# First products of a two-layer trunk: four plain output tiles while x loads, sums of x behind them, pairs in another order

## The chip, the core and the metric

The kernel runs on one core of a Trainium2 chip. The metric is the device time of one execution, in microseconds (us). Five engines work side by side, each with its own queue that is worked off in order: TensorE (PE) multiplies matrices, VectorE (DVE), ScalarE (ACT) and GpSimd (POOL) do elementwise work, and SyncE (SP) issues nearly all DMAs.

## What is computed

A block of 512 tokens x of width 2048 goes through two layers, all in float32. The first is a gated pooling mixer; the second is a latent attention layer that this change does not touch.

```
h = rmsnorm(x, norm_g)
proj = h @ w_in                          # 2048 x 8192
u, gate = proj[..., :4096], proj[..., 4096:]
pooled = causal_mean_pool(u, w) - u      # four groups of 1024, w = 2, 4, 8, 16
y = einsum(pooled, w_group) * scale      # per group 1024 x 1024
y = y * silu(gate)
x = x + y @ w_out
# then shared keys and values, attention with a gate, out projection
```

## The kernel before, in words

Activations lie transposed: 128 channels on the partitions and the 512 tokens along the free axis, so x is 16 tiles (`xT`), and the input product has 64 output tiles of 128 channels, numbers 0 to 31 for u and 32 to 63 for the gate. The rms factor of x is one number per token, so the product runs on x times its gain (`C_GA`) and the factor `ra` is multiplied in afterwards.

Every product is made in split precision. A float32 operand is cast to `hi` (ACT) and its remainder `lo` = value minus hi is made on DVE; three matmuls hi·hi, hi·lo and lo·hi add up in PSUM. In code lines these are a group of three.

The input product saves matmuls by a seven-multiplication scheme for 2x2 blocks (`SEVEN`, `seven`). A **pair** is two output tiles; a step j takes two tiles of x (2j and 2j+1), each in two halves of H = 256 tokens. So a pair and a step make a 2x2 times 2x2 block product, with seven products of 256 columns in place of eight, each in three matmuls: a pair has 8 steps x 7 x 3 = 168 matmuls. It needs sums of weights and sums of x:

- `x_combos(j)` loads two tiles of x, scales them on ACT into a buffer `raw` of eight slots (L275, L277), forms four sums on DVE (L279 to L282), casts seven slots to `xh` (L283) and makes `xl` (L284). These stay for the whole product.
- `w_combos(pair, q)` loads the weights of two steps (L290, two DMAs), forms sums on DVE (L293) and on POOL (L295, L296), casts seven slots (L299) and makes lo (L300). The buffer `raw` has three copies, hi and lo two each.
- `gather` adds the products of a pair up from PSUM into two output tiles and stores them to DRAM (`raws`). The second tile of a pair comes out negated. For u tiles 0 to 7 it applies the pooling window 2 first, which needs `ra`.

The first two pairs, 16 and 17 (gate tiles 32 to 35), run side by side step by step while x is loaded and combined (L353 to L364), in all eight PSUM banks. Then come pairs 18 and 19, then 0 to 15 (u), then 20 to 31 (gates). `squares`, called in pair 18, loads all of x again, squares it on ACT and adds on POOL (L348); `norm_r` in pair 19 makes `ra` from it.

After the product, `pooled_tile` and `y_tile` read `raws` back, group by group, and the group and out products follow (`proj`), with 512-column matmuls at L139, L140 and L141. Their weights are cast at L121 and subtracted at L122.

What sets the order: the code is recorded, and a scheduler with a cost model of its own sorts the instructions of each engine and gives out pool buffers. So instructions stand on an engine in another order than in the code, and wait for semaphores in that order. Memory pools are opened and closed as a stack; a tile in a pool that is opened later waits for the tiles that lay there.

Of the kernel before, what the change touches and what calls it, by code (L numbers as in the profile page):

```python
# [51 lines left out]
def trunk_kernel(  # L52
# [31 lines left out]
    def bt(shape=(P, S), dt=F32R):  # L84
        return bpool.tile(list(shape), dt, tag="b", name="bt")

    def tt_(n=S, dt=F32):
        return tpool.tile([P, n], dt, tag="t", name="tt_")

    def mm():  # L90
        return ps.tile([P, S], F32, tag="mm", name="mm", bufs=3)
# [7 lines left out]
    def f(ap):  # L99
        return ap.bitcast(F32)  # L100

    def dram():
        return dpool.tile([P, S], F32, tag="scr", name="scr", bufs=64)
# [119 lines left out]

    H = 256
    NJ = KD // 2
    raws = [None] * (2 * WA // P)
    ra = [None]

    def pool_tile(src, neg, w):
# [25 lines left out]

    with ExitStack() as c1:
        xcp = c1.enter_context(tc.tile_pool(name="xcp", bufs=NJ))
        epool = c1.enter_context(tc.tile_pool(name="epool", bufs=2))
        w7 = c1.enter_context(tc.tile_pool(name="w7", bufs=2))
        ps7 = c1.enter_context(tc.tile_pool(name="ps7", bufs=2, space=bass.MemoryType.PSUM))  # L260
        xh, xl = [None] * NJ, [None] * NJ

        def raw8():
            return w7.tile([P, 8, H], F32, tag="raw", name="raw", bufs=3)

        def x_combos(j):
            xa, xb_ = tt_(), tt_()
            nc.sync.dma_start(xa, xT[2 * j])
            nc.sync.dma_start(xb_, xT[2 * j + 1])
            h = xcp.tile([P, 7, H], F32R, tag="xh", name="xh")  # L270
            lo = xcp.tile([P, 7, H], F32R, tag="xl", name="xl")
            xh[j], xl[j] = h, lo
            c = raw8()

            A.activation(c[:, 6:8, :].rearrange("p h t -> p (h t)"), xa, AF.Copy,  # L275
                         scale=cs[:, C_GA + 2 * j:C_GA + 2 * j + 1])
            A.activation(c[:, 0:2, :].rearrange("p h t -> p (h t)"), xb_, AF.Copy,  # L277
                         scale=cs[:, C_GA + 2 * j + 1:C_GA + 2 * j + 2])
            V.tensor_tensor(c[:, 2, :], c[:, 6, :], c[:, 7, :], ALU.subtract)  # L279
            V.scalar_tensor_tensor(c[:, 3, :], c[:, 2, :], -1.0, c[:, 1, :], ALU.mult, ALU.subtract)  # L280
            V.scalar_tensor_tensor(c[:, 4, :], c[:, 3, :], -1.0, c[:, 0, :], ALU.mult, ALU.subtract)
            V.tensor_tensor(c[:, 5, :], c[:, 1, :], c[:, 7, :], ALU.subtract)  # L282
            A.copy(h, c[:, 0:7, :])  # L283
            V.tensor_tensor(lo, c[:, 0:7, :], f(h), ALU.subtract)  # L284

        def w_combos(pair, q):

            c = w7.tile([P, 2, 8, P], F32, tag="raw", name="raw", bufs=3)
            for m in range(2):
                nc.sync.dma_start(c[:, :, 2 - 2 * m:4 - 2 * m, :],  # L290
                                  awin[2 * pair + m][:, q * S:(q + 1) * S].rearrange(
                                      "p (j k n) -> p j k n", j=2, k=2))
            V.tensor_tensor(c[:, :, 4:6, :], c[:, :, 0:1, :].broadcast_to([P, 2, 2, P]),  # L293
                            c[:, :, 1:3, :], ALU.add)
            G.tensor_tensor(c[:, :, 6, :], c[:, :, 4, :], c[:, :, 2, :], ALU.add)  # L295
            G.tensor_tensor(c[:, :, 7, :], c[:, :, 6, :], c[:, :, 3, :], ALU.add)  # L296
            hi = w7.tile([P, 2, 7, P], F32R, tag="hi", name="hi")
            lo = w7.tile([P, 2, 7, P], F32R, tag="lo", name="lo")
            A.copy(hi, c[:, :, 1:8, :])  # L299
            V.tensor_tensor(lo, c[:, :, 1:8, :], f(hi), ALU.subtract)  # L300
            return hi, lo

        def banks():
            return [ps7.tile([P, 2, H], F32, tag=f"k{i}", name=f"k{i}") for i in range(4)]


        SEVEN = ((2, 0, 0, 0), (0, 4, 1, 0), (1, 6, 2, 0), (3, 2, 3, 0),
                 (5, 3, 0, 1), (6, 1, 1, 1), (4, 5, 2, 1))

        def seven(ks, w, j):  # L310
            hi, lo = w
            for wi, xi, b, h in SEVEN:
                dst = ks[b][:, h, :]
                first, last = j == 0 and h == 0, j == NJ - 1

                T.matmul(dst, hi[:, j % 2, wi, :], xh[j][:, xi, :], start=first, stop=False,  # L316
                         skip_group_check=True)
                T.matmul(dst, hi[:, j % 2, wi, :], xl[j][:, xi, :], start=False, stop=False,  # L318
                         skip_group_check=True)
                T.matmul(dst, lo[:, j % 2, wi, :], xh[j][:, xi, :], start=False, stop=last,  # L320
                         skip_group_check=True)

        def gather(ks, pair):

            e = epool.tile([P, 7, H], F32, tag="e", name="e")
            A.copy(e[:, 6, :], ks[2][:, 0, :])
            V.tensor_tensor(e[:, 0:2, :], e[:, 6:7, :].broadcast_to([P, 2, H]), ks[0], ALU.add)
            V.tensor_tensor(e[:, 2, :], e[:, 1, :], ks[2][:, 1, :], ALU.add)
            V.tensor_tensor(e[:, 3:6:2, :], e[:, 1:3, :], ks[3][:, 0:1, :].broadcast_to([P, 2, H]), ALU.add)
            V.tensor_tensor(e[:, 4:7:2, :], e[:, 2:4, :], ks[1], ALU.add)  # L330
            for i, v in enumerate((e[:, 0:7:6, :], e[:, 4:6, :])):
                o = 2 * pair + i
                raws[o] = dram()
                if o < 8:
                    nc.sync.dma_start(raws[o], pool_tile(v, i == 1, WINS[0]))
                else:
                    nc.sync.dma_start(raws[o].rearrange("p (h t) -> p h t", h=2), v)

        def squares():
            accs = [tt_(), tt_()]  # L340
            for k in range(KD):
                x = tt_()
                nc.sync.dma_start(x, xT[k])
                if k < 2:
                    A.activation(accs[k], x, AF.Square)
                else:
                    A.activation(x, x, AF.Square)
                    G.tensor_tensor(accs[k % 2], accs[k % 2], x, ALU.add)  # L348
            V.tensor_tensor(accs[0], accs[0], accs[1], ALU.add)
            return accs[0]  # L350


        k0, k1 = banks(), banks()  # L353
        for j in range(NJ):
            x_combos(j)
            if j % 2 == 0:
                wa = w_combos(16, j // 2)
                wb = w_combos(17, j // 2)
                continue
            for i in (j - 1, j):  # L360
                seven(k0, wa, i)
                seven(k1, wb, i)
        gather(k0, 16)
        gather(k1, 17)  # L364
        ss = None
        for pair in (18, 19, *range(16), *range(20, 32)):
            ks = banks()
            for q in range(NJ // 2):
                w = w_combos(pair, q)
                seven(ks, w, 2 * q)  # L370
                seven(ks, w, 2 * q + 1)
            if pair == 18:
                ss = squares()
            if pair == 19:
                p = ps7.tile([P, 2, H], F32, tag="k3", name="k3").rearrange("p h t -> p (h t)")
                ra[0] = norm_r(ss, D, p)
            gather(ks, pair)

    tile_ = dict(reuse_waits="tile")
    wpool = ctx.enter_context(tc.tile_pool(name="wpool", bufs=3, **tile_))  # L380
    apool = ctx.enter_context(tc.tile_pool(name="apool", bufs=32, **tile_))
    bpool = ctx.enter_context(tc.tile_pool(name="bpool", bufs=32, **tile_))
    xpool = ctx.enter_context(tc.tile_pool(name="xpool", bufs=16, **tile_))
    ps = ctx.enter_context(tc.tile_pool(name="ps", bufs=2, space=bass.MemoryType.PSUM, **tile_))


# [2 lines left out]
    def pooled_tile(g, o):  # L389
        x = tt_()  # L390
        nc.sync.dma_start(x, raws[g * 8 + o])
        if g:
            x = pool_tile(x, o % 2 == 1, WINS[g])
        hi, lo = at(), at()
        split(x, hi, lo)
        return hi, lo

    def y_tile(g, o, pooled):
        z = tt_()
        nc.sync.dma_start(z, raws[32 + g * 8 + o])  # L400
        V.scalar_tensor_tensor(z, z, -1.0 if o % 2 else 1.0, ra[0], ALU.mult, ALU.mult)
        A.activation(z, z, AF.Silu)
        acc2 = proj(awg[g, o], 8, pooled)
        c = C_ASC + g * 8 + o
# [499 lines left out]
```

## Time and profile before

| | us |
|---|---|
| median of 3 runs | 1993.39 (1992.2 to 1994.09) |
| the profiled execution | 1993.23 |
| its span, first to last instruction | 1991.4 |
| PE busy | 1941.2 (97%), 11372 matmuls |
| DVE busy | 1289.7 (65%) |
| ACT busy | 815.8 (41%) |
| POOL busy | 299.1 (15%) |

The profile is that of one execution. Busy time counts an instruction from start to end; matmuls overlap, so their pitch (from start to start) is shorter than the time that one is shown with. The granted clock is the share of full speed at which TensorE ran. In rows of the timeline stand start, duration, engine, line, operation, output<-inputs and shape, and in brackets the idle time ahead of it and what ended it. A wait is put down to what came last.

### The profile page before, as it was taken

To read this page: it belongs to the slowest core of one execution; us is meant where nothing else is said; L and a number is where in the kernel's file an instruction comes from. 1 tells how busy PE (TensorE), PEld (TensorE's weight loads), DVE (VectorE), ACT (ScalarE), POOL (GpSimd) and SP (SyncE) were. 2 spreads that over 40 slices of the span, in tenths; PEclk is the share of its full clock that TensorE was granted. 3 is DMA by queue.
4 is the path that set the end of the run, shared out by engine and by line. 5 is a ranking of instruction groups with operands and counts; after the bars stand their busy time and mean duration, and the time that the engine had idled before them with its cause. 6 is when DMAs were issued, how large, how long until landed. Compare 5 with 4: busy or idle time off the path is not lost.

```text
span 1991.4 us, 30647 instructions
## 1 busy us (share of the span) xinstructions
PE 1941.2 (97%) x11372; PEld 1717.5 (86%) x11372; DVE 1289.7 (65%) x2291; ACT 815.8 (41%) x1527; POOL 299.1 (15%) x434
## 2 busy tenths in 40 slices
PE   5699999999999999999999999999999999999999
PEld 5699999999999978888888888888888788878887
DVE  6778866666666589377496567473344878787422
ACT  5433333333333353233333354233244767675221
POOL 2733432222222200000000000000010211110000
PEclk9799999999999999999999999999999999999999
DMA  4534544444444374344344344323332111121632
GB/s 157 175 111 134 168 129 138 128 135 125 135 127 134 121 243 159 106 127 148 112 128 136 107 144 132 94 92 99 96 94 76 51 42 46 50 65 48 211 121 87
DMA packets 167110, 235.53 MB, mean 118 GB/s; under 512 B 14640, under 2 KB 93360, under 8 KB 166960
## 3 DMA queue, kind: packets, MB, share of 16 engines
q1 hardware_dynamic: 166672, 233.37, 37.6%
q8 instruction: 89, 1.46, 0.3%
q14 instruction: 61, 0.50, 0.1%
q10 hardware_dynamic: 288, 0.20, 0.0%
HBM read 208.35 MB, written 25.17 MB: 117 GB/s over the span
## 4 chain that ended last, share of the span: by engine, by line
PE 93%; DVE 3%; DMA 1%; ACT 1%; issue 1%; POOL 0%; SPq 0%; DVEq 0%; ACTq 0%; POOLq 0%
PE mm L141 16%; PE mm L139 16%; PE mm L140 16%; PE k L320 10%; PE k L316 10%; PE k L318 10%; PE sc L696 3%; PE mm L570 1%; PE mm L571 1%; PE mm L572 1%; DMA raw<-awin 1%; PE tr L655 1%; PE mm L592 1%; PE mm L590 1%; PE mm L591 1%; PE tr L715 1%
## 5 line engine op out<-in xcount | busy, mean ns | idle before, releaser
L316 PE MATMUL k<-xh,hi 128*128 128x256 f32 x1792 | 493.7, 287 | 31.3 <-ACT hi L299 31.1
L318 PE MATMUL k<-xl,hi 128*128 128x256 f32 x1792 | 495.7, 286 | 0.9 <-DVE xl L284 0.8
L121 ACT CAST whi<-raw 128x512 fp32r<-128x512 f32 (+2 forms) x421 | 256.1, 611 | 537.0 <-PE mm L140 461.6
L320 PE MATMUL k<-xh,lo 128*128 128x256 f32 x1792 | 450.3, 287 | 4.9 <-DVE lo L300 4.9
L122 DVE TENSOR_TENSOR wlo<-raw,whi 128x512 fp32r<-128x512 f32 (+2 forms) x421 | 282.1, 672 | 225.6 <-ACT whi L121 221.8
L299 ACT CAST hi<-raw 128x1792 fp32r<-128x1792 f32 x128 | 216.2, 1690 | 406.9 <-PE k L320 260.5
L300 DVE TENSOR_TENSOR lo<-raw,hi 128x1792 fp32r<-128x1792 f32 x128 | 266.2, 2080 | 179.2 <-ACT hi L299 179.2
L316 PEld LDWEIGHTS k<-xh,hi 128*128 128x128 f32 x1792 | 348.0, 195 | 32.3 <-ACT hi L299 31.9
L318 PEld LDWEIGHTS k<-xl,hi 128*128 128x128 f32 x1792 | 349.5, 195 | 1.3 <-DVE xl L284 1.3
L141 PE MATMUL mm<-bt,wlo 128*128 128x512 f32 x860 | 335.5, 390 | 0.0
L139 PE MATMUL mm<-bt,whi 128*128 128x512 f32 x860 | 334.7, 389 | 0.0
L140 PE MATMUL mm<-bt,whi 128*128 128x512 f32 x860 | 334.5, 389 | 0.0
L320 PEld LDWEIGHTS k<-xh,lo 128*128 128x128 f32 x1792 | 321.6, 195 | 6.9 <-DVE lo L300 6.4
L139 PE MATMUL mm<-at,whi 128*128 128x512 f32 x516 | 202.1, 393 | 2.6 <-ACT whi L121 2.5
L141 PE MATMUL mm<-at,wlo 128*128 128x512 f32 x516 | 202.3, 392 | 1.7 <-DVE wlo L122 1.7
L140 PE MATMUL mm<-at,whi 128*128 128x512 f32 x516 | 202.3, 392 | 0.0
L141 PEld LDWEIGHTS mm<-bt,wlo 128*128 128x128 f32 x860 | 161.5, 188 | 34.2 <-issue 0.5
L139 PEld LDWEIGHTS mm<-bt,whi 128*128 128x128 f32 x860 | 161.5, 188 | 33.7 <-issue 0.2
L140 PEld LDWEIGHTS mm<-bt,whi 128*128 128x128 f32 x860 | 161.5, 188 | 33.5
L295 POOL TENSOR_TENSOR raw<-raw 128x256 f32<-128x256 f32 x128 | 107.0, 836 | 421.8 <-DVE raw L293 408.1
L141 PEld LDWEIGHTS mm<-at,wlo 128*128 128x128 f32 x516 | 97.4, 189 | 23.8 <-DVE wlo L122 3.6
L139 PEld LDWEIGHTS mm<-at,whi 128*128 128x128 f32 x516 | 97.5, 189 | 23.0 <-ACT whi L121 3.0
(1148 smaller groups left out, 2434.3 us busy)
## 6 DMA issues: line engine op xcount, KB each, us to landing
raw<-awin SPq DMA_DIRECT2D x256, 256.0 KB, 3.3
raw<-awo SPq DMA_DIRECT2D x128, 256.0 KB, 2.7
raw<-bwin SPq DMA_DIRECT2D x80, 256.0 KB, 2.8
raw<-awg SPq DMA_DIRECT2D x64, 256.0 KB, 2.9
raw<-bwo SPq DMA_DIRECT2D x59, 256.0 KB, 2.8
scr<-e SPq DMA_DIRECT2D x56, 256.0 KB, 2.6
raw<-wkvb SPq DMA_DIRECT2D x32, 256.0 KB, 3.1
raw<-wqb SPq DMA_DIRECT2D x32, 192.0 KB, 2.4
```

The lines of the kernel that those rows point to most:

```text
L121: A.copy(hi[:, :n], raw[:, :n])
L122: V.tensor_tensor(lo[:, :n], raw[:, :n], f(hi[:, :n]), ALU.subtract)
L139: T.matmul(dst, wh, xh, start=first, stop=False)
L140: T.matmul(dst, wh, xl, start=False, stop=False)
L141: T.matmul(dst, wl, xh, start=False, stop=last)
L295: G.tensor_tensor(c[:, :, 6, :], c[:, :, 4, :], c[:, :, 2, :], ALU.add)
L299: A.copy(hi, c[:, :, 1:8, :])
L300: V.tensor_tensor(lo, c[:, :, 1:8, :], f(hi), ALU.subtract)
L316: T.matmul(dst, hi[:, j % 2, wi, :], xh[j][:, xi, :], start=first, stop=False, skip_group_check=True)
L318: T.matmul(dst, hi[:, j % 2, wi, :], xl[j][:, xi, :], start=False, stop=False, skip_group_check=True)
L320: T.matmul(dst, lo[:, j % 2, wi, :], xh[j][:, xi, :], start=False, stop=last, skip_group_check=True)
L696: T.matmul(s[:, 0:n], l, r, start=(j == 0), stop=(j == 4))
```

## The change

- **Gate tiles 32 to 35 as plain products.** In a new loop over the eight steps, two tiles of x are loaded straight into slots 2, 7 and 0, 1 of `raw` (`x_load`), in pieces of 256 tokens, and the weights of four tiles for this step into `hraw` (four DMAs of 128 KB). `x_parts` scales x in place, casts slots 0 to 2 (`xh`) and slot 7 (`h12`, a tile of a pool that is closed after the loop) and makes their remainders. The weights are split two tiles at a time. Then, for each of the four tiles, nine matmuls per step: six of 256 columns and three of 512 (L371 to L373), into one PSUM bank for each tile. The four tiles are copied out by ACT and stored; none is negated.
- **Sums of x behind them.** `x_sums` makes the four sums, their cast (L291) and remainder (L292) for the pairs that follow. The slots are numbered anew, so `SEVEN` has other indices for x.
- **Order of pairs:** 18 to 31 (the other gates), then 0 to 15 (u). A set `neg` notes which tiles are negated.
- **Squares spread out:** two tiles of x per pair in the first eight pairs, added on DVE instead of POOL (L394); the norm follows in the ninth.
- **Pools:** `w7` and `epool` track reuse tile by tile; the pool of small tiles `tt_` is opened after the plain loop and again after the product, in place of one that stays open.

```diff
+        def x_load(j):
+            c = w7.tile([P, 8, H], F32, tag="raw", name="raw", bufs=3)
+            nc.sync.dma_start(c[:, 2:8:5, :], xT[2 * j].rearrange("p (h t) -> p h t", h=2))
+            nc.sync.dma_start(c[:, 0:2, :], xT[2 * j + 1].rearrange("p (h t) -> p h t", h=2))
+            return c
+        def x_parts(j, c, hp):
...
+            A.activation(c[:, 2:8:5, :], c[:, 2:8:5, :], AF.Copy, scale=cs[:, C_GA + 2 * j:C_GA + 2 * j + 1])
+            A.activation(c[:, 0:2, :], c[:, 0:2, :], AF.Copy, scale=cs[:, C_GA + 2 * j + 1:C_GA + 2 * j + 2])
+            A.copy(h[:, 0:3, :], c[:, 0:3, :])
+            V.tensor_tensor(lo[:, 0:3, :], c[:, 0:3, :], f(h[:, 0:3, :]), ALU.subtract)
+            split(c[:, 7, :], h12, l12)
+        def x_sums(j, c):
+            h, lo = xh[j], xl[j]
+            V.tensor_tensor(c[:, 3:5, :], c[:, 1:3, :], c[:, 7:8, :].broadcast_to([P, 2, H]), ALU.subtract)
+            V.scalar_tensor_tensor(c[:, 5, :], c[:, 4, :], -1.0, c[:, 1, :], ALU.mult, ALU.subtract)
+            V.scalar_tensor_tensor(c[:, 6, :], c[:, 5, :], -1.0, c[:, 0, :], ALU.mult, ALU.subtract)
+            A.copy(h[:, 3:7, :], c[:, 3:7, :])
+            V.tensor_tensor(lo[:, 3:7, :], c[:, 3:7, :], f(h[:, 3:7, :]), ALU.subtract)
...
-        k0, k1 = banks(), banks()
-        for j in range(NJ):
-            x_combos(j)
-            if j % 2 == 0:
-                wa = w_combos(16, j // 2)
-                wb = w_combos(17, j // 2)
-                continue
-            for i in (j - 1, j):
-                seven(k0, wa, i)
-                seven(k1, wb, i)
-        gather(k0, 16)
-        gather(k1, 17)
-        for pair in (18, 19, *range(16), *range(20, 32)):
...
-            if pair == 18:
-                ss = squares()
+        accs = [ps7.tile([P, 2, H], F32, tag=f"k{i}", name=f"k{i}") for i in range(4)]
+            hp = c2.enter_context(tc.tile_pool(name="hp", bufs=2, **tile_))
+            for j in range(NJ):
+                c = x_load(j)
+                raw = hp.tile([P, 4, 2, P], F32, tag="hraw", name="hraw")
+                hi = w7.tile([P, 4, 2, P], F32R, tag="hi", name="hi")
+                lo = w7.tile([P, 4, 2, P], F32R, tag="lo", name="lo")
+                for o in range(4):
+                    nc.sync.dma_start(raw[:, o, :, :], awin[32 + o][:, 2 * j * P:2 * (j + 1) * P].rearrange(
+                        "p (k n) -> p k n", k=2))
+                h12, l12 = x_parts(j, c, hp)
+                for o in (0, 2):
+                    split(raw[:, o:o + 2], hi[:, o:o + 2], lo[:, o:o + 2])
+                x_sums(j, c)
+                a, b = xh[j], xl[j]
+                for o in range(4):
+                    for dst, k, h, l in ((accs[o][:, 0, :], 0, a[:, 2, :], b[:, 2, :]),
+                                         (accs[o][:, 1, :], 0, h12, l12),
+                                         (accs[o], 1, a[:, 0:2, :], b[:, 0:2, :])):
+                        first = j == 0 and h is not h12 and k == 0
+                        T.matmul(dst, hi[:, o, k, :], h, start=first, stop=False, skip_group_check=True)
+                        T.matmul(dst, hi[:, o, k, :], l, start=False, stop=False, skip_group_check=True)
+                        T.matmul(dst, lo[:, o, k, :], h, start=False, stop=j == NJ - 1 and k == 1,
+                                 skip_group_check=True)
...
+        for n, pair in enumerate((*range(18, 32), *range(16))):
...
+            if n < 8:
+                square(2 * n)
+                square(2 * n + 1)
+            if n == 8:
+                V.tensor_tensor(sq[0], sq[0], sq[1], ALU.add)
...
+                ra[0] = norm_r(sq[0], D, p)
...
+    tp[0] = ctx.enter_context(tc.tile_pool(name="tpool2", bufs=6, **tile_))
```

More of the change, by code (lines that the diff above doesn't have):

```diff
@@ L85, in bt @@
         return bpool.tile(list(shape), dt, tag="b", name="bt")
+    tp = [None]
     def tt_(n=S, dt=F32):
-        return tpool.tile([P, n], dt, tag="t", name="tt_")
+        return tp[0].tile([P, n], dt, tag="t", name="tt_")
     def mm():
@@ L225, in trunk_kernel @@
     NJ = KD // 2
+    tile_ = dict(reuse_waits="tile")
     raws = [None] * (2 * WA // P)
+    neg = set()
     ra = [None]
@@ L257, in trunk_kernel @@
         xcp = c1.enter_context(tc.tile_pool(name="xcp", bufs=NJ))
-        epool = c1.enter_context(tc.tile_pool(name="epool", bufs=2))
-        w7 = c1.enter_context(tc.tile_pool(name="w7", bufs=2))
+        w7 = c1.enter_context(tc.tile_pool(name="w7", bufs=2, **tile_))
         ps7 = c1.enter_context(tc.tile_pool(name="ps7", bufs=2, space=bass.MemoryType.PSUM))
         xh, xl = [None] * NJ, [None] * NJ
[L263 to L269, printed above, removed]
+        def x_load(j):
[4 more added lines that the diff above has]
+        def x_parts(j, c, hp):
             h = xcp.tile([P, 7, H], F32R, tag="xh", name="xh")
@@ L272, in x_combos @@
             xh[j], xl[j] = h, lo
[L273 to L284, printed above, removed]
+            h12 = hp.tile([P, H], F32R, tag="h12", name="h12", bufs=NJ)
+            l12 = hp.tile([P, H], F32R, tag="l12", name="l12", bufs=NJ)
+            A.activation(c[:, 2:8:5, :], c[:, 2:8:5, :], AF.Copy, scale=cs[:, C_GA + 2 * j:C_GA + 2 * j + 1])
[3 more added lines that the diff above has]
+            split(c[:, 7, :], h12, l12)
+            return h12, l12
+        def x_sums(j, c):
[5 more added lines that the diff above has]
+            V.tensor_tensor(lo[:, 3:7, :], c[:, 3:7, :], f(h[:, 3:7, :]), ALU.subtract)
         def w_combos(pair, q):
@@ L304, in banks @@
             return [ps7.tile([P, 2, H], F32, tag=f"k{i}", name=f"k{i}") for i in range(4)]
-        SEVEN = ((2, 0, 0, 0), (0, 4, 1, 0), (1, 6, 2, 0), (3, 2, 3, 0),
-                 (5, 3, 0, 1), (6, 1, 1, 1), (4, 5, 2, 1))
+        SEVEN = ((2, 0, 0, 0), (0, 6, 1, 0), (1, 2, 2, 0), (3, 4, 3, 0),
+                 (5, 5, 0, 1), (6, 1, 1, 1), (4, 3, 2, 1))
         def seven(ks, w, j):
@@ L333, in gather @@
                 raws[o] = dram()
+                if i:
+                    neg.add(o)
                 if o < 8:
@@ L337, in gather @@
                     nc.sync.dma_start(raws[o].rearrange("p (h t) -> p h t", h=2), v)
[L339 to L350, printed above, removed]
@@ new lines, in trunk_kernel @@
+        with ExitStack() as c2:
+            hp = c2.enter_context(tc.tile_pool(name="hp", bufs=2, **tile_))
[21 more added lines that the diff above has]
+                                 skip_group_check=True)
@@ new lines, in trunk_kernel @@
+        epool = c1.enter_context(tc.tile_pool(name="epool", bufs=2, **tile_))
+        tp[0] = c1.enter_context(tc.tile_pool(name="tpool1", bufs=6, **tile_))
+        for o in range(0, 4, 2):
+            e = epool.tile([P, 7, H], F32, tag="e", name="e")
+            for i in range(2):
+                v = e[:, 2 * i:2 * i + 2, :]
+                A.copy(v, accs[o + i])
+                raws[32 + o + i] = dram()
+                nc.sync.dma_start(raws[32 + o + i].rearrange("p (h t) -> p h t", h=2), v)
@@ L367, in trunk_kernel, with square @@
+        sq = [tt_(), tt_()]
+        def square(k):
+            x = tt_()
+            nc.sync.dma_start(x, xT[k])
+            if k < 2:
+                A.activation(sq[k], x, AF.Square)
+            else:
+                A.activation(x, x, AF.Square)
+                V.tensor_tensor(sq[k % 2], sq[k % 2], x, ALU.add)
+        for n, pair in enumerate((*range(18, 32), *range(16))):
             ks = banks()
@@ L371, in trunk_kernel @@
                 seven(ks, w, 2 * q + 1)
-            if pair == 18:
-                ss = squares()
-            if pair == 19:
+            if n < 8:
[3 more added lines that the diff above has]
+                V.tensor_tensor(sq[0], sq[0], sq[1], ALU.add)
                 p = ps7.tile([P, 2, H], F32, tag="k3", name="k3").rearrange("p h t -> p (h t)")
-                ra[0] = norm_r(ss, D, p)
+                ra[0] = norm_r(sq[0], D, p)
             gather(ks, pair)
-    tile_ = dict(reuse_waits="tile")
     wpool = ctx.enter_context(tc.tile_pool(name="wpool", bufs=3, **tile_))
@@ L392, in pooled_tile @@
         if g:
-            x = pool_tile(x, o % 2 == 1, WINS[g])
+            x = pool_tile(x, g * 8 + o in neg, WINS[g])
         hi, lo = at(), at()
@@ L400, in y_tile @@
         nc.sync.dma_start(z, raws[32 + g * 8 + o])
-        V.scalar_tensor_tensor(z, z, -1.0 if o % 2 else 1.0, ra[0], ALU.mult, ALU.mult)
+        V.scalar_tensor_tensor(z, z, -1.0 if 32 + g * 8 + o in neg else 1.0, ra[0], ALU.mult, ALU.mult)
         A.activation(z, z, AF.Silu)
```

2 lines of the change are left out of this document (removed).

## The prediction

> **What bounds the kernel now.** I read first the busy times in five stretches (columns: stretch, length, then busy time and instruction count of PE, weight loads, DVE, ACT, POOL, then granted clock, DMA share and GB/s).
>
> ```profile
> 0.00:15.30 15.30, 0.00 (x0) 0.00 (x0) 5.74 (x12) 6.03 (x6) 5.13 (x8) 1.00 0.65 219
> 15.30:91.00 75.70, 53.98 (x344) 51.19 (x344) 60.87 (x62) 44.69 (x48) 43.06 (x31) 0.83 0.51 157
> 91.00:698.50 607.50, 607.42 (x5034) 606.71 (x5034) 414.48 (x398) 207.34 (x147) 194.28 (x244) 1.00 0.43 132
> 698.50:708.00 9.50, 6.20 (x16) 4.40 (x15) 8.94 (x16) 6.19 (x12) 0.00 (x0) 0.64 0.64 203
> 708.00:1991.00 1283.00, 1273.57 (x5981) 1055.25 (x5979) 799.63 (x1807) 551.57 (x1315) 56.65 (x152) 1.00 0.34 108
> ```
>
> From 91 us on TensorE hardly rests; what can be won lies ahead. The pitch of a 256-column matmul comes from a stretch without pauses (the first row below: 550/4579 = 0.1201 us), that of a 512-column one from one of three lines that take turns (second row: 100/148/3 = 0.2252 us).
>
> ```profile
> 100.00:650.00 550.00, 550.00 (x4579) 549.37 (x4579) 382.45 (x370) 191.59 (x136) 177.69 (x225) 1.00 0.43 134
> 900.00:1000.00 100.00, 57.23 (x148) 27.60 (x147) 1.00 0.42 131
> ```
>
> The input product's 32 pairs x 168 = 5376 matmuls are worth 645.7 us, and it ends at 698.5: 52.8 us are lost, 91 - 344 x 0.1201 = 49.7 of them before 91 us. The waits up to 100 us say on what (who, for whom, us, times, longest):
>
> ```profile
> POOL raw L295 <- DVE raw L293: 33.5, 6, 10.8
> ...
> PE k L316 <- ACT hi L299: 31.1, 5, 15.3
> ACT hi L299 <- POOL raw L296: 13.5, 3, 5.1
> ```
>
> PE waits for the weights' cast, which waits for POOL's two sums, which wait for DVE's. Later POOL also adds the squares of x, and both it and DVE slow down: a row of each (DVE's subtraction takes 2.01 elsewhere, below).
>
> ```profile
> 66.57 3.07 POOL L348 TENSOR_TENSOR tt__864<-tt__864,tt__883 128x512 f32<-128x512 f32 x1
> ...
> 71.44 3.10 DVE L300 TENSOR_TENSOR lo<-raw,hi 128x1792 fp32r<-128x1792 f32 x1
> ```
>
> **Part 1: four plain tiles in place of pairs 16 and 17.** No weight sum stands ahead of a matmul any more, and the first tiles need four slots of x, not seven. ACT's start shows it, before and then after (88 and 101 are x's buffers, hi_116 the weights with their sums, hi_92 the weights alone):
>
> ```order
> L275 ACT_TABLE_LOAD
> L275 ACTIVATE raw_101<-tt__95,cs_69 128x512
> L277 ACTIVATE raw_101<-tt__96,cs_69 128x512
> L283 CAST xh_99<-raw_101 128x1792
> L299 CAST hi_116<-raw_110 128x1792
> L275 ACTIVATE raw_136<-tt__130,cs_69 128x512
> ```
>
> ```order
> L279 ACT_TABLE_LOAD
> L279 ACTIVATE raw_88<-raw_88,cs_66 128x2x256
> L280 ACTIVATE raw_88<-raw_88,cs_66 128x512
> L145 CAST h12_100<-raw_88 128x256
> L281 CAST xh_98<-raw_88 128x768
> L145 CAST hi_92<-hraw_91 128x512 x2
> L279 ACTIVATE raw_153<-raw_153,cs_66 128x2x256
> L280 ACTIVATE raw_153<-raw_153,cs_66 128x512
> L291 CAST xh_98<-raw_88 128x1024
> ```
>
> The cast of x's sums (L291) has moved behind the weights' cast and behind the next x. The first matmul waits for the first hi_92. When does that come? The start in the trace, and the pitch of casts on ACT and subtractions on DVE where they stand back to back:
>
> ```profile
> 4.24 1.28 ACT L275 ACT_TABLE_LOAD   x1 [4.24 <-DMA tt__95<-xT]
> 5.54 0.72 ACT L275 ACTIVATE raw<-tt__95,cs 128x512 f32<-128x512 f32 x1
> 6.17 0.71 ACT L277 ACTIVATE raw<-tt__96,cs 128x512 f32<-128x512 f32 x1
> ...
> 15.31 0.58 PE L316 MATMUL k<-xh,hi 128*128 128x256 f32 x1 [15.31 <-ACT hi L299]
> ...
> 31.90 1.67 ACT L299 CAST hi<-raw 128x1792 fp32r<-128x1792 f32 x1
> 33.47 0.72 ACT L275 ACTIVATE raw<-tt__363,cs 128x512 f32<-128x512 f32 x1
> ...
> 698.93 0.62 ACT L144 CAST at<-tt__7476 128x512 fp32r<-128x512 f32 x1
> 699.45 0.62 ACT L144 CAST at<-tt__7482 128x512 fp32r<-128x512 f32 x1
> ...
> 34.06 2.01 DVE L300 TENSOR_TENSOR lo<-raw,hi 128x1792 fp32r<-128x1792 f32 x1
> 36.00 0.41 DVE L281 SCALAR_TENSOR_TENSOR raw<-raw 128x256 f32<-128x256 f32 x1
> 36.33 0.41 DVE L279 TENSOR_TENSOR raw<-raw 128x256 f32<-128x256 f32 x1
> ```
>
> Starts give ACT 0.52 us for 512 columns and 1.57 for 1792, so 0.31, 0.73 and 0.94 for 256, 768 and 1024; DVE 0.33 for 256 and 1.94 for 1792, so 0.60, 0.87 and 1.14 for 512, 768 and 1024. x now arrives in 1 KB pieces where it came in 2 KB ones. Two stretches of the opening, of 2 KB and then of 1 KB pieces, show what that does:
>
> ```profile
> 3.00:5.00 2.00, 0.00 (x0) 0.00 (x0) 0.16 (x1) 0.76 (x1) 0.00 (x0) 1.00 1.07 390
> 7.00:9.00 2.00, 0.00 (x0) 0.00 (x0) 1.00 (x3) 0.91 (x1) 0.00 (x0) 1.00 0.93 259
> ```
>
> The first 256 KB take 1.0 us instead of 0.67; with the constants' load beside them I put the table load 0.5 later, at 4.7. Then 1.3 + 2 x 0.63 + 0.31 + 0.73 + 0.52, and 0.2 for the hand-over: the first matmul at 9.0 us (bounds 7.8, if the pieces cost nothing and casts overlap, and 11, if weights land late). The Trainium skill (DMA: Bandwidth & Descriptors, Specifications) names 512 B as the least transfer at line rate, by which x's smaller pieces would cost nothing and the time would be 0.5 us less; the trace disagrees, 259 against 390 GB/s.
>
> The work: 4 tiles x 8 steps x (6 of 256 and 3 of 512) = 192 x 0.1201 + 96 x 0.2252 = 44.7 us, where the two pairs took 336 x 0.1201 = 40.4. It runs at half rate first, as at the old start, and after the pause at the phase change:
>
> ```profile
> 19.46 0.41 PE L320 MATMUL k<-xh,lo 128*128 128x256 f32 x1
> 19.67 0.41 PE L316 MATMUL k<-xh,hi 128*128 128x256 f32 x1
> ...
> 21.54 0.28 PE L316 MATMUL k<-xh,hi 128*128 128x256 f32 x1
> ...
> 701.16 0.80 PE L139 MATMUL mm<-at,whi 128*128 128x512 f32 x1 [2.54 <-ACT whi L121]
> ```
>
> From 15.31 to 21.54 the pitch is about 0.21 (19.46 to 19.67): 6.2 x (1 - 0.1201/0.21) = 2.7 us lost (bounds 1.7 and 5.4, half to twice).
>
> Can the others keep up with 5.6 us a step? ACT: 1.26 (x scaled) + 0.31 + 0.73 (its parts) + 1.04 (weights) + 0.94 (sums) = 4.3. DVE: 0.33 + 0.87 + 1.20 for the same, 0.60 + 0.66 + 1.14 for the sums: 4.8. DMA: 1 MB at 259 GB/s, 4.0. All are under it, and x's sums are hidden beneath the plain products. I charge 1.5 us for pauses (bounds 0 and the late feed below).
>
> **Part 2: squares.** They leave POOL and go to DVE, 14 adds at 0.60 = 8.4 us. POOL before, then DVE after (tt are square tiles, raw and lo weights):
>
> ```order
> L348 TENSOR_TENSOR tt__864<-tt__864,tt__883 128x512
> L348 TENSOR_TENSOR tt__863<-tt__863,tt__887 128x512
> L348 TENSOR_TENSOR tt__864<-tt__864,tt__891 128x512
> L348 TENSOR_TENSOR tt__863<-tt__863,tt__895 128x512
> L348 TENSOR_TENSOR tt__864<-tt__864,tt__899 128x512
> L348 TENSOR_TENSOR tt__863<-tt__863,tt__903 128x512
> L295 TENSOR_TENSOR raw_655<-raw_655 128x2x128
> ```
>
> ```order
> L308 TENSOR_TENSOR lo_798<-raw_791,hi_797 128x1792
> L394 TENSOR_TENSOR tt__629<-tt__629,tt__1301 128x512
> L301 TENSOR_TENSOR raw_915<-raw_915 128x2x256
> L394 TENSOR_TENSOR tt__630<-tt__630,tt__1305 128x512
> L394 TENSOR_TENSOR tt__629<-tt__629,tt__1531 128x512
> L394 TENSOR_TENSOR tt__630<-tt__630,tt__1535 128x512
> L308 TENSOR_TENSOR lo_870<-raw_863,hi_869 128x1792
> ```
>
> POOL's sums no longer queue behind six adds; up to four adds stand between two of DVE's subtractions, over the first two pairs. A weight tile lasts 42 x 0.1201 = 5.04 us on PE and takes 1.94 + 0.60 of DVE, so 2.5 us are free: four adds take 2.4. What covers them is that PE has a tile in reserve. The norm's chain loaded DVE as heavily, and PE did not pause:
>
> ```profile
> 115.00:150.00 35.00, 35.00 (x287) 34.37 (x287) 32.27 (x34) 11.13 (x8) 12.04 (x13) 1.00 0.39 119
> ```
>
> So nothing is charged here; uncovered it is the second rival.
>
> **Part 3: order of pairs, signs, pools, new waits.** Sign flags cost no instruction. Three of the four copies of the finished plain tiles stand on ACT between pair 18's first two casts and wait for the last plain matmul: 3 x 0.52, cast 1.57 and subtraction 1.94 make 5.1 us, against 5.04 of the first weight tile and 8 matmuls (1.0) that need no subtraction. Covered; without cover, 1 us. On SP the first square's load waits for the same matmul, as its tile lies in the closed pool's memory; behind it queue the four stores and pair 19's loads, while pair 18's four loads stand ahead: 4 x 5.04 = 20 us of cover. The phase change keeps its shape (the last pair's gather, then the first casts), and its 9.5 us are kept, plus or minus 2.7 for the clock's return.
>
> **The sum.** First matmul 9.0, half rate 2.7, plain work 44.7, pauses 1.5, 30 pairs x 168 x 0.1201 = 605.3 and the norm's 0.9: the product ends at 664.1 instead of 698.5. The profiled execution took 1993.23 us, its span 1991.4; less 34.4, that is 1958.8, so 1959. The median of the runs, 1993.39, is 0.2 from it.
>
> **Rivals.** *Late feed.* The weights' buffer pair is reloaded only after the subtraction. Opening rows, of four loads' issue and of one slow landing:
>
> ```profile
> 36.10 5.05 SPq L290 DMA_DIRECT2D raw<-awin  x4
> tt__229<-xT SPq DMA_DIRECT2D x1, 256.0 KB, 6.0
> ```
>
> With both, the loop is 5.05 + 6.0 + 1.04 + 1.2 = 13.3 us for two steps, 6.6 a step: 7 x 1.0 more, and two returns to half rate, 5.4: 1971. Against it: these are its slowest rows together. The Trainium skill (TensorE: Matmul & The Clock Gate, What's actually happening) has the half rate return after an idle window of about 3.4 us, which would leave 1966 for this case; the row at 701.16 disagrees, as half rate followed 2.54 us.
>
> *Squares uncovered.* 8.4 + 2.7 = 11.1 if POOL slows DVE as at 71.44; I put 1962 to 1970. Against it is the 35 us row.
>
> *No earlier start* (the change not doing what it says): first matmul at 15.3, 1965. For it, the same table load and first load lead; against, POOL's 13.5 us are out of the chain.
>
> *Slower: the clock stays at half* through the plain products. They would last 44.7 longer, less the 2.7 charged: 2001. It decides if nearly every window holds a pause, as in 15.3 to 91 (mean clock 0.83, and 344 matmuls in 75.7 us). Against: at half rate a step lasts 11 us, and feeding takes 4.8, so the pauses that would hold it there vanish.
>
> **Chances.** Forecast 0.69 (1953 to 1964: first matmul 7.8, half rate 1.7, no pauses, phase change 2.7 better; upward likewise), late feed 0.13, squares 0.10, no earlier start 0.05, half clock 0.03. The range 1953 to 1970 takes in all but late feed's upper half, half clock and the tails. A measurement here tells 0.2%, 4 us, from no change. Faster 0.95, same 0.02 (late feed far beyond its price), slower 0.03.
>
> **Right or wrong.** Right if the first matmul starts near 9 us, L371 to L373 are done by about 58, PE is at full count (0.12 a matmul) from there, and the first matmul after the phase change comes near 667. Wrong if PE waits in the plain products on the hi cast for the load of hraw (late feed), on L308 in the first two pairs after (squares), or if half rate lasts past 20 us.

## The result, and the profile after

The kernel after took 1963.12 us in the median of four runs (1961.67 to 1964.71), the kernel before 1993.03 beside it: a ratio of 0.985 (95% interval 0.9833 to 0.9867), 29.9 us less. The forecast was 1959, with a range of 1953 to 1970. The profiled execution of after took 1961.67 us, its span is 1959.9.

The page's busy times of after, then the same kind of windows as were shown of before (stretch, length, busy time and count of PE, weight loads, DVE, ACT, POOL, then granted clock, DMA share, GB/s):

```profile
PE 1933.3 (99%) x11324; PEld 1707.0 (87%) x11324; DVE 1280.2 (65%) x2305; ACT 815.1 (42%) x1553; POOL 262.9 (13%) x404
```

```profile
0.00:8.46 8.46, 0.00 (x1) 0.01 (x1) 2.07 (x8) 4.22 (x7) 0.20 (x4) 1.00 0.78 228
8.46:55.30 46.84, 46.84 (x288) 42.54 (x289) 41.88 (x65) 34.90 (x55) 5.65 (x5) 1.00 0.57 177
55.30:92.00 36.70, 32.98 (x263) 31.72 (x262) 28.50 (x28) 22.07 (x26) 15.89 (x13) 1.00 0.71 230
92.00:666.90 574.90, 574.67 (x4782) 573.95 (x4782) 399.64 (x384) 196.93 (x140) 184.48 (x232) 1.00 0.43 133
666.90:676.50 9.60, 5.81 (x18) 4.22 (x17) 8.97 (x16) 7.47 (x14) 0.00 (x0) 0.82 0.62 187
676.50:1959.90 1283.40, 1273.03 (x5979) 1054.56 (x5977) 799.09 (x1807) 549.54 (x1314) 56.68 (x152) 1.00 0.34 108
```

The second row is the plain stage: PE is busy in all of it. The third is the only one in which PE rests: its 263 matmuls are worth 31.6 us at a pitch of 0.1201, of 36.7. From 92 us to the end the rows are those of before, moved up. The waits up to 110 us (who, for whom, us, times, longest) say for what PE rested:

```profile
PE k L371 <- ACT hi L145: 8.5, 1, 8.5
PE k L328 <- DVE lo L308: 3.7, 5, 1.6
```

The first is the start; 31.1 us of waits for the weights' cast in the first 100 us of before have gone. The second is new: the matmuls with `lo` wait for DVE's subtraction. By the starts of successive matmuls there are six such gaps between 61.4 and 91.8 us, 4.7 us in all over the pitch. All sixteen squares stand there, at 60 to 93 us. The scheduler has pulled them together, though the code hands them out over eight pairs. Around two of the gaps, on ACT, DVE and PE in turn:

```profile
68.12 0.63 ACT L393 ACTIVATE tt__1071<-tt__1071 128x512 f32<-128x512 f32 x1 [4.27 <-DMA tt__1071<-xT]
68.78 0.63 ACT L393 ACTIVATE tt__1075<-tt__1075 128x512 f32<-128x512 f32 x1
69.31 1.68 ACT L307 CAST hi<-raw 128x1792 fp32r<-128x1792 f32 x1
...
71.03 2.02 DVE L308 TENSOR_TENSOR lo<-raw,hi 128x1792 fp32r<-128x1792 f32 x1 [0.20 <-ACT hi L307]
72.97 0.69 DVE L394 TENSOR_TENSOR tt__629<-tt__629,tt__1301 128x512 f32<-128x512 f32 x1
73.57 0.69 DVE L301 TENSOR_TENSOR raw<-raw 128x512 f32<-128x512 f32 x1
74.18 0.69 DVE L394 TENSOR_TENSOR tt__630<-tt__630,tt__1305 128x512 f32<-128x512 f32 x1
74.78 1.23 DVE L394 TENSOR_TENSOR tt__629<-tt__629,tt__1531 128x512 f32<-128x512 f32 x1
75.94 1.23 DVE L394 TENSOR_TENSOR tt__630<-tt__630,tt__1535 128x512 f32<-128x512 f32 x1
77.08 2.01 DVE L308 TENSOR_TENSOR lo<-raw,hi 128x1792 fp32r<-128x1792 f32 x1
...
79.15 0.62 PE L328 MATMUL k<-xh,lo 128*128 128x256 f32 x3 [0.75 <-DVE lo L308]
```

ACT stands 4.27 us at a square's load, with a weight tile's cast (69.31) queued behind the squares. The subtraction at 71.03 starts as soon as this cast has ended, and PE waits 0.8 us for it: no addition has a part in that gap. For the gap that ends at 79.15, DVE has four additions and one of the weights' sums ahead of the subtraction at 77.08 as well.

### The profile page after: what moved, and what is told of

Its sections match the earlier page's. It is cut to its first block, busy times and chain, and to the rows that moved or that the text cites. A ratio compares the mean times of both kernels' runs of the same rounds, so it can differ in the third digit from the quotient of the medians.

```text
span 1959.9 us, 30545 instructions
## 1 busy us (share of the span) xinstructions
PE 1933.3 (99%) x11324; PEld 1707.0 (87%) x11324; DVE 1280.2 (65%) x2305; ACT 815.1 (42%) x1553; POOL 262.9 (13%) x404
## 4 chain that ended last, share of the span: by engine, by line
PE 93%; DVE 3%; DMA 2%; issue 1%; ACT 1%; SPq 0%; DVEq 0%; ACTq 0%
PE mm L142 16%; PE mm L140 16%; PE mm L141 16%; PE k L328 9%; PE k L324 9%; PE k L326 9%; PE sc L728 3%; PE mm L604 1%; PE mm L602 1%; PE mm L603 1%; PE tr L687 1%; PE mm L622 1%; PE mm L624 1%; PE mm L623 1%; DVE lo L308 1%
## 5 line engine op out<-in xcount | busy, mean ns | idle before, releaser
L324 PE MATMUL k<-xh,hi 128*128 128x256 f32 x1680 | 460.1, 283 | 0.1
L326 PE MATMUL k<-xl,hi 128*128 128x256 f32 x1680 | 460.0, 283 | 0.0
L328 PE MATMUL k<-xh,lo 128*128 128x256 f32 x1680 | 418.1, 284 | 3.9 <-DVE lo L308 3.9
L307 ACT CAST hi<-raw 128x1792 fp32r<-128x1792 f32 x120 | 202.8, 1690 | 373.5 <-PE k L328 258.2
L308 DVE TENSOR_TENSOR lo<-raw,hi 128x1792 fp32r<-128x1792 f32 x120 | 248.9, 2074 | 158.5 <-ACT hi L307 158.5
L324 PEld LDWEIGHTS k<-xh,hi 128*128 128x128 f32 x1680 | 322.5, 192 | 0.3 <-ACT hi L307 0.3
L326 PEld LDWEIGHTS k<-xl,hi 128*128 128x128 f32 x1680 | 322.5, 192 | 0.0
L328 PEld LDWEIGHTS k<-xh,lo 128*128 128x128 f32 x1680 | 296.7, 192 | 5.6 <-DVE lo L308 5.1
L303 POOL TENSOR_TENSOR raw<-raw 128x256 f32<-128x256 f32 x120 | 101.3, 844 | 437.3 <-DVE raw L301 414.7
```

## The experiments

Two questions were open: how much each part of the change brings, and what it is about the squares that makes PE wait. Times are medians; the ratio is to the kernel before, measured beside it.

**One part alone.** The kernel after, with the squares of before (in one go, added on POOL) and its order of pairs:

```
-                V.tensor_tensor(sq[k % 2], sq[k % 2], x, ALU.add)
-
-        for n, pair in enumerate((*range(18, 32), *range(16))):
+        def squares():
...
+                    G.tensor_tensor(accs[k % 2], accs[k % 2], x, ALU.add)
...
+        for pair in (18, 19, *range(16), *range(20, 32)):
```

> The changed kernel with the squares and the order of pairs of before: 16 loads and squares in one go in pair 18, added on POOL. Theory A, the two parts add up: at 46 us, ahead of the squares, before had lost 25.8 us (15.3 to the first matmul, 10.5 over half of the opening's matmuls), so 36 for the whole opening and about 16 of 52 for the squares. The plain products then save 36 - 8.5 - 2.4 - 4.3 = 21 and the 16 stay: about 1972 us. Theory B, the squares cost so much only beside the opening, where DVE had x's sums and the weights' as well: about 1964, with under 6 us of waits on PE after the plain products. The recorded forecast says nothing on the split.

1971.31 us (ratio 0.9891, 0.9876 to 0.9905). The windows row of 50 to 100 us shows POOL busy for 41 of 50, and PE's waits up to 130 us are 10.2 where after has 3.7:

```profile
50.00:100.00 50.00, 42.38 (x320) 40.63 (x319) 28.44 (x19) 24.04 (x29) 40.96 (x28) 0.97 0.63 199
```

```profile
PE k L328 <- DVE lo L308: 7.8, 7, 2.0
PE k L324 <- ACT hi L307: 2.4, 2, 2.0
```

And the kernel before with nothing but the new squares and the new order (pairs 16 and 17 stay on sums):

```
-                    G.tensor_tensor(accs[k % 2], accs[k % 2], x, ALU.add)
...
-        for pair in (18, 19, *range(16), *range(20, 32)):
...
+                V.tensor_tensor(sq[k % 2], sq[k % 2], x, ALU.add)
...
+        for n, pair in enumerate((*range(18, 32), *range(16))):
```

> The kernel before with the squares as in the changed one (two tiles a pair, added on DVE) and its order of pairs; pairs 16 and 17 still run side by side on sums. Theory A: of the 16 us for the squares all but 5 go, about 1982 us. Theory B: they are dear because the opening fills DVE, which now has the adds too: 1988 or more. First matmul at 15.3 under both.

1989.61 us (0.9983, 0.9974 to 0.9992): theory B's figure, though the first matmul came at 14.4 us and not at 15.3. PE's waits up to 130 us are still mostly those of pairs 16 and 17:

```profile
PE k L316 <- ACT hi L299: 19.4, 6, 14.4
PE k L316 <- DVE e L327: 5.8, 1, 5.8
PE k L320 <- DVE lo L300: 5.8, 7, 1.3
```

So the plain tiles alone bring 21.7 us, the squares alone 3.4, both together 29.9. The parts do not add up: theory A of the first run had its time right and its premise wrong. Once the plain tiles stand, moving the squares off POOL is worth 8.2. Some of that is clock: in the profiled execution with POOL's squares the granted clock was 0.50 at 92 to 94 us, where after has 1.00.

**What the sums of x are worth behind the products.** The kernel after with x's sums made ahead of its cast, in one cast and one subtraction of seven slots, as before:

```
-            A.copy(h[:, 0:3, :], c[:, 0:3, :])
...
+            V.tensor_tensor(c[:, 3:5, :], c[:, 1:3, :], c[:, 7:8, :].broadcast_to([P, 2, H]), ALU.subtract)
...
+            A.copy(h, c[:, 0:7, :])
...
-                x_sums(j, c)
```

> The changed kernel with x's sums made ahead of the plain products: one cast and one subtraction of seven slots of x, as before, so that x is not ready until its four sums are. Theory A, after the first step PE is the bound with some 1 us a step to spare, so only the start moves: the cast of 1792 in place of 768 (0.84 us) and three sums (1.3) come ahead of most of step 0; 2 to 3 us, 1965 to 1966. Theory D, putting the sums behind is what keeps PE fed: waits in every step and the half rate, 8 us or more, above 1971.

1968.83 us (0.9876, 0.986 to 0.9893), between the figures of the two theories, so neither is right. The first matmul starts at 10.86 instead of 8.46, and PE waits in the plain stage, where after never does (L374, for x's lo):

```profile
PE k L373 <- ACT xh L284: 10.9, 1, 10.9
PE k L331 <- DVE lo L311: 4.9, 5, 2.0
PE k L374 <- DVE xl L285: 2.2, 2, 1.3
```

**Are the gaps the squares' at all?** The kernel after with two of the sixteen squares (fourteen are left out):

```
-            if n < 8:
+            if n < 1:
```

> The changed kernel, leaving 14 of the 16 squares out (ra is made from the first two tiles of x alone). Theory A, the waits of PE for lo in the first pairs after the plain products (six gaps, 4.7 us) come from squares that stand ahead of weight casts on ACT and ahead of subtractions on DVE: under 1 us of them is left, the span falls by about 4, to 1956, the time to about 1959. Theory C, they come from weight loads that are late because raw has three buffers only: 3 us or more are left, 1962 or above.

1958.53 us (0.9827, 0.9813 to 0.9842). Theory A: the only wait of PE up to 130 us is the start; all six gaps are gone. The product ends at 663.2 (after: 666.9; forecast: 664.1).

```profile
PE k L371 <- ACT hi L145: 8.3, 1, 8.3
```

**Which work of the squares?** First the additions on POOL, with everything else as in after:

```
-                V.tensor_tensor(sq[k % 2], sq[k % 2], x, ALU.add)
+                G.tensor_tensor(sq[k % 2], sq[k % 2], x, ALU.add)
```

> The kernel after, with the fourteen additions of squares on GpSimd instead of VectorE. Theory A (GpSimd makes sums of the weights that the casts wait for, and an addition there lasts 1.07 us or more): its queue grows, the waits of the matmuls in the first eight pairs grow from 4.7 to 8 to 15 us, and the time is 1966 to 1974. Rival B (VectorE is the engine that is short, GpSimd has 0.50 of its time left): the waits fall below 3 us and the time is 1959 to 1962.

1970.23 us (0.9885, 0.9869 to 0.99): theory A. POOL is busy for 43.34 of 54.7 us (after 23.49), PE waits for casts too, and there are eleven gaps, 9.9 us over the pitch.

```profile
55.30:110.00 54.70, 46.53 (x355) 44.29 (x354) 31.13 (x22) 25.76 (x29) 43.34 (x30) 0.97 0.57 184
```

```profile
PE k L328 <- DVE lo L308: 6.9, 7, 1.4
PE k L324 <- ACT hi L307: 1.2, 3, 0.4
```

Then without the additions, and without the loads (the fourteen additions kept, ScalarE squaring a running sum):

```
-                V.tensor_tensor(sq[k % 2], sq[k % 2], x, ALU.add)
```

> The kernel after without the fourteen additions: each square is still loaded and made on ScalarE, but only the first two count, so the norm is that of two of the sixteen rows of tiles. Theory A1 (the waits on lo come of ScalarE, whose cast of a weight tile stands behind squares that wait 2 to 4 us for their loads): the waits on L308 stay at 3.5 us or more, and the time is 1962 to 1963.5. Theory A2 (they come of VectorE, whose additions of 1.23 us stand ahead of a subtraction): the waits fall to 1.5 us or less, and the time is 1959 to 1960. Between the two, each has a share.

```
-            nc.sync.dma_start(x, xT[k])
...
-                A.activation(x, x, AF.Square)
+                A.activation(x, sq[k % 2], AF.Square, scale=1e-3)
```

> The kernel after without the last fourteen loads of x for the squares: ScalarE squares the running sum instead (scaled), and VectorE adds as before, so the norm is not that of x. Theory A2 (VectorE's additions alone make the waits): they stay at 3.5 us or more, 1962 to 1963.5. Theory S (loads and additions each make a share, since leaving out the additions took 3 of the 4.6 us): 1 to 3 us of waits are left and the time is 1959 to 1962.

1960.0 us (0.9831, 0.9816 to 0.9847) and 1959.94 (0.9832, 0.9816 to 0.9849). Waits up to 130 us, of the first (two rows) and of the second:

```profile
PE k L328 <- DVE lo L308: 1.1, 2, 0.8
PE k L324 <- ACT hi L307: 0.6, 1, 0.6
```

```profile
PE k L328 <- DVE lo L308: 0.6, 2, 0.3
```

The gaps are 2.2 us without the additions, 1.0 without the loads, 4.7 with both. So neither alone makes them. A2 had its numbers right in the first run and falls by the second, where it said 3.5 us of waits or more; theory S has the time right, but 0.6 us of waits are under the 1 to 3 that it said. One limit: without the loads the additions came two to a weight tile, not up to four; but DVE was as busy from 61 to 92 us (28.00 of 31, after 26.96, below), and PE hardly rested:

```profile
61.00:92.00 31.00, 30.65 (x256) 30.45 (x255) 28.00 (x26) 18.75 (x21) 14.84 (x12) 1.00 0.41 131
```

**Moving them.** Three kernels were to move the squares. In the first, ScalarE's and VectorE's part comes a pair after its loads; in the second the squares begin with the fifth pair:

```
+            if 0 < n < 9:
+                square()
+                square()
...
+                load(2 * n)
+                load(2 * n + 1)
```

> The kernel after, with the loads of two squares where they were, but ScalarE's and VectorE's work on them a pair later, about 17 us, when the loads have long landed. Theory A1 (ScalarE's wait for these loads): the waits on L308 fall to 1.5 us or less, and the time is 1959 to 1960.5. Theory A2 (VectorE's additions): they stay at 3.5 us or more, and the time is 1962 to 1963.5.

```
-            if n < 8:
-                square(2 * n)
...
+            if 4 <= n < 12:
+                square(2 * n - 8)
```

> The kernel after, with the same two squares a pair, but beginning with the fifth pair on sums (about 140 us) instead of the first (55 us), and the norm behind the thirteenth. Theory R (the squares only cost because the weight tiles have no lead over TensorE in the first pairs; ScalarE waits there for loads, and later it waits for TensorE to give tiles back, 97.7 us of 92 to 300): the waits on L308 go, none longer than 0.5 us, the span is 1956.5 to 1957.5 and the time 1958 to 1960. Theory W (sixteen squares on these engines cost 3 to 5 us wherever they stand): the waits move to 140 to 300 us, and the time is 1962 to 1964.

1962.67 us (0.9844, 0.9828 to 0.9859) and 1963.85 (0.9854, 0.9839 to 0.9869), no different from after. Both failed as experiments. In the first kernel the first and the last square stand on ACT at 59.27 and 89.11 us; of the second kernel these are the rows:

```profile
60.57 0.63 ACT L391 ACTIVATE tt__629<-tt__1731 128x512 f32<-128x512 f32 x1 [2.41 <-DMA tt__1731<-xT]
...
90.41 0.63 ACT L393 ACTIVATE tt__3343<-tt__3343 128x512 f32<-128x512 f32 x1 [0.80 <-DMA tt__3343<-xT]
```

Nothing moved: the squares' inputs depend on x alone, and the scheduler put them where it had put them in after. So neither A1 nor W was tested by these two. The third ties each square to a weight tile, by a tiny addition that reads both:

```
+            V.tensor_tensor(dum, x[:, 0:1], f(w[1])[:, 0, 0, 0:1], ALU.add)
...
+                if n < 4:
+                    square(4 * n + q, w)
```

> The kernel after, with one square for each weight tile over four pairs (instead of two at the end of each of eight pairs), all in a single square tile, whose next load starts only once VectorE has made the weight tile's lo. Theory A (the waits on lo in the first pairs come of the squares standing in pairs in the queues ahead of a cast and a subtraction): at most 1 us of waits on L308 is left and the time is 1958.5 to 1960.5. Rival B (any square work in this stage costs what it costs, 0.3 us of waits for each square, wherever it stands): the waits stay at 4 to 5 us, all within four pairs, and the time is 1962 to 1964.

1964.57 us (0.9855, 0.9837 to 0.9872). The squares did spread, over 55 to 137 us, and three gaps of 4.1 us in all came at 97, 118 and 140 us. B's numbers, but not its reason. ACT stands at a square's load with the cast behind it, DVE at a weight load:

```profile
92.16 0.63 ACT L395 ACTIVATE sx<-sx 128x512 f32<-128x512 f32 x1 [4.23 <-DMA sx<-xT]
92.70 1.68 ACT L307 CAST hi<-raw 128x1792 fp32r<-128x1792 f32 x1
```

```profile
95.41 0.69 DVE L301 TENSOR_TENSOR raw<-raw 128x512 f32<-128x512 f32 x1 [1.82 <-DMA raw<-awin]
96.02 2.02 DVE L308 TENSOR_TENSOR lo<-raw,hi 128x1792 fp32r<-128x1792 f32 x1
```

With one buffer for all squares, each load starts late and ACT waits for it: the pacing itself took the feed's lead. So this run does not price a square.

**Held back by data.** The last one forces the whole burst, as dense as it was, to a later place: a column of the first four square tiles is written from a late pair's `lo`.

```
+            if k < 4:
+                V.tensor_scalar(x[:, 0:1], f(w[1])[:, 0, 0, 0:1], 1.0, None, ALU.mult)
             nc.sync.dma_start(x, xT[k])
...
-            if n < 8:
...
+            if 4 <= n < 12:
```

> In the two earlier kernels (a pair later, four pairs later) the squares did not move: the scheduler put them at 60 to 93 us as before, whatever their place in the code, so those two told nothing of the cause. Here they are held back by data: the first four square tiles get one column written by VectorE (four instructions of one element a row) from the last weight tile's lo of the fifth to sixth pair, so that all sixteen squares stand about 100 us later, in as dense a burst, 14 additions on VectorE beside up to sixteen loads. Theory R (the feed has no lead over TensorE just behind the plain products, and that is why the squares cost there; from 100 us on ScalarE waits for TensorE to free tiles): no waits on L308 at 55 to 100 us, under 1 us of them later, span 1956.5 to 1958, time 1958 to 1960. Theory W (a dense burst of additions and loads costs 3 to 5 us wherever it stands): the waits move to the burst, time 1962 to 1965.

1959.4 us (0.9829, 0.9815 to 0.9842; runs of 1958.41 to 1959.53, where the lowest of after is 1961.67). It is faster than both kernels. The squares stand at 156 to 201 us, and fourteen of them within 25 us. Up to four additions, and two sums of a pair's products, still stand between two subtractions, and ACT still waits for loads (ACT's rows first, then DVE's):

```profile
176.55 0.63 ACT L395 ACTIVATE tt__1961<-tt__1961 128x512 f32<-128x512 f32 x1 [2.41 <-DVE lo L308]
...
188.45 0.63 ACT L395 ACTIVATE tt__2657<-tt__2657 128x512 f32<-128x512 f32 x1 [2.99 <-DMA tt__2657<-xT]
```

```profile
179.90 2.01 DVE L308 TENSOR_TENSOR lo<-raw,hi 128x1792 fp32r<-128x1792 f32 x1
181.83 0.68 DVE L301 TENSOR_TENSOR raw<-raw 128x512 f32<-128x512 f32 x1
...
183.86 1.23 DVE L396 TENSOR_TENSOR tt__629<-tt__629,tt__2423 128x512 f32<-128x512 f32 x1
...
186.54 2.01 DVE L308 TENSOR_TENSOR lo<-raw,hi 128x1792 fp32r<-128x1792 f32 x1
```

But PE waits little; up to 230 us, but for the start:

```profile
PE k L328 <- DVE lo L308: 1.9, 3, 1.3
```

The 1.3 us wait ends at 62.2 us, where no square has begun. It belongs to the seam between the plain products and the pairs. The second weight tile's `lo` is ready near 62.2 in this kernel, in after and with two squares: its subtraction starts at about 60.1, as VectorE stands ahead of it at a later weight tile's load until about 59.5. The pairs start at 54.84, 55.53 and 56.22, so that PE waits 1.4, 0.6 and 0 us over the pitch. The squares' own share in after is then 4.0 us. Here the burst leaves 0.6 us of waits (three gaps, 1.2 us over the pitch). Two stretches of 31 us show the same load on DVE and on the DMAs, and PE at 30.48 where it had 27.28; first this kernel, then after:

```profile
170.00:201.00 31.00, 30.48 (x252) 30.07 (x251) 28.30 (x32) 16.89 (x21) 10.38 (x10) 1.00 0.73 225
```

```profile
61.00:92.00 31.00, 27.28 (x217) 26.07 (x216) 26.96 (x27) 18.70 (x22) 14.35 (x11) 1.00 0.69 223
```

R's time came true, and the burst's waits stayed under 1 us; the 1.3 us at 62.2 it had ruled out. Place is worth 2.8 us, 4.0 against 1.2. R's reason does not stand as it was put, that the feed has no lead in the first pairs. In after, the loads that ACT waits for from 55 to 97 us are all the squares' own. In the kernel with two squares, ACT's largest item in the same 55 to 97 us is that PE must give tiles back (first row), as it is in after from 100 to 260 us (second row):

```profile
ACT hi L307 <- PE k L328: 16.8, 5, 3.4
```

```profile
ACT hi L307 <- PE k L328: 77.6, 23, 3.8
```

And in after the weight tile that starts on PE at 66.31 us has its `hi` ready 3.95 us and its `lo` 2.71 us before the first matmul that reads each; in the quiet stretch from 125 to 225 us it is 3.15 and 2.05. So the reserve was there, and the next tile had used it up (0.05 us for `lo`, and a gap).

What uses it up can be read from the casts. In the quiet stretch a weight tile's cast starts 0.2 us after the first matmul of the tile before. In after four casts in a row start 3.0 to 3.9 us after it (69.31, 74.37, 80.50 and 87.25), though the sums that they read had been ready for 3.9 to 5.2 us: ACT stood at the squares. In the held-back burst five casts start 0.8 to 2.9 us after it (178.13 to 200.62). Why ACT holds them up less there is not shown. One thing that differs is that VectorE waits for two weight loads at the head of the burst in after (4.67 and 3.00 us, ending at 59.46 and 67.56), and for none in the held-back burst.

**The order of pairs** was tried alone, with u's pairs in the middle:

```
-        for n, pair in enumerate((*range(18, 32), *range(16))):
+        for n, pair in enumerate((*range(18, 26), *range(16), *range(26, 32))):
```

> The kernel after with the order of the pairs 18 to 25, 0 to 15, 26 to 31, so that the tiles to be pooled come earlier and gate tiles last. The prediction charged this order with nothing: within 1 us of the kernel after, 1962 to 1964.5. Rival: the pooled pairs (VectorE 46.5 of 50 us at 400 to 450) bring waits when they stand earlier, or the phase change waits for a tile made last: 1965 or more.

1962.99 us (0.9849, 0.9835 to 0.9864), 0.1 from after: between these two orders the time does not change, as charged.

## Why the prediction was right, and where it was wrong

The mechanism was right: POOL's chain left the opening, and most of the time lost ahead of 91 us came back. By its steps, in spans (forecast 1957.0, measured 1959.9):

- **First matmul**: 9.0 said, 8.46 measured. The half microsecond for x's smaller pieces was wrong; ACT's table load, which waits for x, started at 4.23, as before (4.24). Besides, only the even tiles of x come in 1 KB pieces; the odd ones keep 2 KB. By the Trainium skill's line rate from 512 B on (DMA: Bandwidth & Descriptors, Specifications), the pieces cost nothing, and this start agrees. The 259 against 390 GB/s that I read as the price of the pieces were two stretches of the opening that differed in more than that: in after 7 to 9 us, with weights in 1 KB pieces, moves 344 GB/s.
- **Plain stage**: 44.7 of work, 2.7 for half rate and 1.5 for pauses make 48.9 said; 47.1 measured (8.46 to 55.53). The matmuls came at full pitch from 12.8 us, so half rate cost 2.2, and there were no pauses. ACT, DVE and DMA kept up, as the prediction's account of a step said. With x's sums ahead of the products the kernel is 5.7 us slower: 2.4 at the first matmul, 2.2 in waits for x's lo (L374), the rest mostly in the first pairs.
- **Pairs on sums**: 606.2 said with the norm, 611.4 measured (55.53 to 666.93). This is the step that failed: "What covers them is that PE has a tile in reserve", and "So nothing is charged here". The reserve was there, but the squares used it up. The step weighed them on DVE alone; ACT's part, squares that wait for loads with weight casts behind them, was put at nothing. ACT waits 14.4 us for these loads, in nine waits from 55 to 90 us. The row that was to prove the cover (115 to 150 us, DVE busy for 32.27 of 35) has DVE as busy, but no squares to load, and ACT busy for 11.13 of 35. The additions were also priced too low: 0.60 each, while six of the fourteen, those beside POOL's sums, last 1.2. In all the squares cost 4.0 us here, and 0.6 fell to the seam. Held back, the burst costs 1.2 and the product ends at 663.7, where 664.1 was forecast; that these two are near is chance, since there the pairs start 3.1 us sooner than forecast and take 2.7 longer.
- **The rival** named this, and with it a sign of being wrong that came true: PE waits on L308 in the first two pairs after. It came at 4.0 us of its 11.1: there was no return to half rate, and DVE's subtractions in these gaps took 2.01 to 2.17, not 3.10.
- **Order of pairs and phase change**: nothing charged; 0.1 us for the order, and from the product's end to the last instruction 1293.0 us, as before.

The errors, -0.5, -1.8 and +5.2, make the +2.9 of the span: that the first two hide near half of the third is luck. The median lies 1.5 us above the profiled execution, the fastest of the four.

Left open: how the squares' 4.0 us split between additions and loads (leaving out either gives back more than half, so the shares are not to be added up), and what makes the same burst cheaper 110 us later.

## What to carry to other kernels

A cover must be read on every engine that the work passes through. Here side work was weighed on VectorE, while ScalarE held up TensorE's feed: its short squares, waiting for loads, delayed the weight casts that stood behind them on the engine. A stretch that proves a cover must hold the same work, its loads too.

Whether a feeder has a lead is read from what it waits for: the consumer (a lead) or its loads (none). Read that from a run without the side work, or the side work's own waits are taken for the feeder's.

Here the scheduler placed work by what its data depend on, not by its line; look at the timeline before believing that an edit moved anything.

## What the hardware showed besides

DVE's addition of 128x512 takes 0.69 us alone (72.97, above), and 1.23 beside POOL's sums of 1.07 (74.78 and 75.94; POOL's start at 74.39 and 75.54, and take 0.74 at 68.39). The addition at 74.18, begun before POOL's, still takes 0.69. The Trainium skill (SBUF — State Buffer, Who interferes with whom) says that a VectorE instruction with two inputs in SBUF contends with a GpSimd instruction that reads SBUF; these rows agree.

The end of half rate at the start differed between executions that all began at 8.3 to 8.5 us. By the pitch of the matmuls it came at 11.3 us in the held-back kernel, 12.8 in after and 14.5 with two squares, and the pairs start in that order (54.84, 55.53, 56.22). Half rate also came back in one kernel and not in another with like gaps: with the squares four pairs later in the code (gaps of 5.0 us) the granted clock was 0.51 at 94 to 96 us, in after (4.7 us) it was 1.00.

Half rate did not follow the pause at the phase change at once. In after, TensorE came back at full pitch after 2.54 us, and the slow stretch of 3.4 us (pitch 0.43, 672.20 to 672.62) began only with the next wait:

```profile
669.62 0.50 PE L140 MATMUL mm<-at,whi 128*128 128x512 f32 x1 [2.54 <-ACT whi L122]
669.96 0.40 PE L141 MATMUL mm<-at,whi 128*128 128x512 f32 x1
671.61 0.79 PE L142 MATMUL mm<-at,wlo 128*128 128x512 f32 x1 [1.25 <-DVE wlo L123]
672.20 0.63 PE L140 MATMUL mm<-at,whi 128*128 128x512 f32 x1
672.62 0.63 PE L141 MATMUL mm<-at,whi 128*128 128x512 f32 x1
```

Before and the held-back kernel have 6.8 us of half rate there, and all three take 1292.7 to 1293.0 us from the product's end to the last instruction: at this place the clock is not what sets the time.
